# A sixth buffer for split weights, with two weight sums written over loaded weights, in a decoder trunk on one core

## The chip, the cores and the metric

The kernel runs on one core of one Trainium2 chip. The metric is the device time of one execution in microseconds; the kernel before takes 2459.61 us, the median of three runs (2458.16 to 2460.76). One further execution was taken with the profiler on: 2458.1 us, of which the span from the first to the last profiled instruction is 2456.3 us. The rows of the profile are of that execution.

The engines by their names in the profile: PE multiplies matrices (PEld loads its stationary operand), DVE does elementwise work on vectors, ACT copies, casts and evaluates functions, POOL is a slower general engine, and SP issues DMA transfers.

## What is computed

Two layers on 256 tokens of width 2048, all in float32. Layer 0 is RetNet retention (8 heads) and an MLP with squared ReLU; layer 1 is latent attention over a shared key and value (16 heads) and an MLP of the same form.

```python
x = x + retention(rms_norm(x, norm_mix[0]), w_in, w_out, cos, sin)
x = x + square(relu(rms_norm(x, norm_mlp[0]) @ w1)) @ w2
k_nope, k_pe, v = mla_shared_kv(rms_norm(x, kv_norm_in), ...)
x = x + mla_attention(rms_norm(x, norm_mix[1]), ..., k_nope, k_pe, v)
x = x + square(relu(rms_norm(x, norm_mlp[1]) @ w1)) @ w2
```

The weights are some 480 MB and are read once. Nearly all time goes into products of 256 tokens with weight matrices.

## The kernel before

**Split products.** A float32 number is split into a high part (a rounding cast on ACT, line 216) and a low part (number minus high part, a subtraction on DVE, line 217). A product of two split matrices takes three matmuls: high by high, high by low, low by high (lines 409 to 411). Each matmul has 512 columns.

**Quads.** A weight matrix is cut into blocks of 256 by 1024; `quad` (from line 321) handles one. One transfer of 1 MB on SP's queue (line 324) brings it into a tile `raw`, of which there are three. It holds four pieces of 512 columns in the order B11, B22, B12, B21. The tokens stand in two halves and the inner dimension in two, so a quad multiplies two by two pieces by two by two. There are two kinds:

- A plain quad, an *eight*, splits `raw` in two parts of 1024 columns and does eight products (24 matmuls).
- A quad with sums, a *seven*, uses Winograd's form of Strassen's scheme: seven products (21 matmuls) on B11, B22, B21 and four sums of weights, u1 = B11+B12, u3 = B22+B12, u2 = u1+B22 and u4 = u2+B21 (with the signs put into the activations). DVE makes u1 and u3 in one addition (line 363), u2 (line 372) and u4 (line 373), and the four parts are then split in the order (B11, B22), (B21), (u2, u4), (u1, u3). The products follow in that order: p1, c12; c11; c21, p6; p5, p7.

Which quads of a GEMM are sevens is written out by hand (`SEVEN`, `ODD`, `HEAD` and so on): three or four of eight in most GEMMs, two in some.

**Buffers.** Each part has a tile `wh` and a tile `wl` of 1024 columns; there are five of each. The sums of one quad take both places of the tag `us`. A cast into `wh` waits until PE has used the part five places before; a load waits until the last reader of the `raw` three loads before is done; the first sum waits until `us` is free.

**Pairs.** `gemm_pair` runs eight quads into eight PSUM banks (four `acc`, two `tp`, and one double bank for p6 and p7) and then hands them to `pair_out`, where ACT copies c22, c12, c11, c21, p1 and p5 and DVE adds p6 and p7. The next GEMM takes those banks again. There are 16 such pairs for the first MLP matrices (names `u_`) and 16 for the second (`d_`), seven for gates and values of retention (`rp_`), four for its output (`ro_`), and one each in attention's query (`dqp_`) and output (`wop_`). Other GEMMs go through `stream` (line 242), with splits of the same size and without sums.

**Order of the work.** Python code emits everything unrolled; short tasks (evictions, transposes, normalisation, softmax) are put on a list with a due time counted in quads (`later`, `tick`). A scheduler then orders each engine's queue by emission order and readiness and makes the waits. `queued_behind` adds an order between two instructions of one engine: in a seven, the first sum goes behind the first low part of the quad before, and the first low parts go behind the last sum.

**Small things that the change touches.** `gains`, `cst` (inverse frequencies for the rotations, mask of three blocks of 128 columns, identity) and `gpe` are constants loaded at the start, the last two in `start` (lines 684 to 697). `sincos` computes the rotation tables on POOL in a chain of some 25 instructions; `rope_tab` serves the retention heads, `pe_tabs` and the rotated key `kpe_t` serve attention. `small` is a ring of 36 tiles for row statistics, `f2k` a ring of 14 tiles of 2 KB per partition for all else.

Of the kernel before, what the change touches and what calls it, by code (L numbers as in the profile page):

```python
# [35 lines left out]
P = 128  # L36
NT = 2
# [12 lines left out]

G_MIX0, G_MLP0, G_KV, G_MIX1, G_MLP1 = 0, 16, 32, 48, 64
G_CKV, G_CQ, G_KN, G_QN, G_ALL = 80, 84, 96, 97, 98
C_INVR, C_INVM, C_MASK, C_ID, C_ALL = 0, 128, 160, 544, 672

MAGIC = 1.5 * 2.0**23
MAGIC_HI = 1.5 * 2.0**35
# [10 lines left out]
def yoco(ctx: ExitStack, tc: tile.TileContext, a):  # L67
# [5 lines left out]
        return pool.tile([P, *shape], dtype, tag="f2k", bufs=14, name=name)  # L73

    def small(w, name):
        return pool.tile([P, w], F32, tag="small", bufs=36, name=name)

    def shaped(t, shape):
        v = t[:, : math.prod(shape)]
# [33 lines left out]


    gains = pool.tile([P, G_ALL], F32, name="gains")
    cst = pool.tile([P, C_ALL], F32, name="cst")
    pos_i = pool.tile([P, NT], I32, name="pos_i")
    gpe = pool.tile([P, 2 * ROPE], F32, name="gpe")
    nc.scalar.dma_start(gains, a["gains"])
    ident = cst[:, C_ID : C_ID + P]  # L120
    mask = cst[:, C_MASK : C_MASK + 3 * P]
    neg_half = pool.tile([P, 16], F32, name="neg_half")
    nc.gpsimd.memset(neg_half, -0.5)
    warm = small(1, "warm")
    nc.scalar.copy(warm, neg_half[:, 0:1])
# [112 lines left out]
    def stream(w, chunk, cols, name, use, done=None, before=None):  # L238

        raw = pool.tile([P, 2048], F32, tag="raw", bufs=3, name=f"{name}_raw")  # L240
        if before is None:
            nc.sync.dma_start(raw[:, :cols], w[chunk])
        n = cols // 2
        for half in range(2):
            wh = pool.tile([P, 1024], F32R, tag="wh", bufs=5, name=f"{name}_wh{half}")
            wl = pool.tile([P, 1024], F32R, tag="wl", bufs=5, name=f"{name}_wl{half}")
# [74 lines left out]
    def quad(w, chunk, x, mm, name, split_ends=False):  # L321

        raw = pool.tile([P, 2048], F32, tag="raw", bufs=3, name=f"{name}_raw")
        nc.sync.dma_start(raw, w[chunk])
        v, more = x

        def a(t, k):
            return [v[:, k, i, t * P : (t + 1) * P] for i in range(2)]

        def s(n):  # L330
            return [more[:, n // 2, i, n % 2 * P : (n % 2 + 1) * P] for i in range(2)]

        def parts(src, n, part, after=None):
            wh = pool.tile([P, 1024], F32R, tag="wh", bufs=5, name=f"{name}_wh{part}")
            wl = pool.tile([P, 1024], F32R, tag="wl", bufs=5, name=f"{name}_wl{part}")
            low = low_part[0] = split(wh[:, : n * 512], wl[:, : n * 512], src)
            if after is not None:
                queued_behind(low, after)
            if part == 0:
                first_low[0] = low  # L340
            return [[i[:, j * 512 : (j + 1) * 512] for i in (wh, wl)] for j in range(n)]

        if more is None:
            b11, b22 = parts(raw[:, 0:1024], 2, 0)
            if not split_ends:
                mm("c11", a(0, 0), b11)
                mm("c21", a(1, 0), b11)
                mm("c12", a(0, 1), b22)
# [12 lines left out]
            return  # L361
        u = [pool.tile([P, 2, 512], F32, tag="us", bufs=2, name=f"{name}_u{i}") for i in range(2)]
        first_sum = nc.vector.tensor_tensor(
            u[0], raw[:, 0:1024].rearrange("p (i n) -> p i n", i=2),
            raw[:, 1024:1536].unsqueeze(1).to_broadcast([P, 2, 512]), op=ALU.add,
        )
        if first_low[0] is not None:
            queued_behind(first_sum, first_low[0])
        if ahead[1] is not None:
            queued_behind(first_sum, ahead[1])  # L370
            ahead[1] = None
        nc.vector.tensor_tensor(u[1][:, 0], u[0][:, 0], raw[:, 512:1024], op=ALU.add)
        summed_up = nc.vector.tensor_tensor(u[1][:, 1], u[1][:, 0], raw[:, 1536:], op=ALU.add)  # L373
        b11, b22 = parts(raw[:, 0:1024], 2, 0, summed_up)
        mm("p1", a(0, 0), b11)
        mm("c12", s(3), b22)
        (b21,) = parts(raw[:, 1536:], 1, 1, summed_up)
        mm("c11", a(0, 1), b21)
        u2, u4 = parts(u[1].rearrange("p i n -> p (i n)"), 2, 2)
        mm("c21", a(1, 1), u4)  # L380
        mm("p6", s(2), u2)
        u1, u3 = parts(u[0].rearrange("p i n -> p (i n)"), 2, 3)
        mm("p5", s(1), u1)
        mm("p7", s(0), u3)

    def gemm_pair(w, chunk0, act, kinds, name, done, order=None, inner=None, ends=False):

# [216 lines left out]
        return finish  # L604

    scale = (NOPE + ROPE) ** -0.5
    rope_tab = pool.tile([P, 2, S], F32, name="rope_tab")
    pe_tabs = [[pool.tile([P, 2, ROPE], F32, name=f"petab{t}{i}") for i in range(2)] for t in range(NT)]
    gqn = pool.tile([P, 1], F32, name="gqn")

    def mla_tables():
        sm = mla_sc[0](no_turn[0])
# [13 lines left out]

    def ret_tables():
        nc.vector.tensor_copy(pos_f, pos_i)
        ret_sc.append(sincos(cst[:, C_INVR : C_INVR + 128], 128, "tr"))

    def scale_tables():
        r0.extend(x_rstd(ss0, "n0"))
# [51 lines left out]
    def start(half):  # L684
        first_inputs(half)
        if half == 4:
            nc.sync.dma_start(pos_i, a["pos"])
            nc.sync.dma_start(cst, a["cst"])
            nc.sync.dma_start(gpe, a["gpe"])
        if half == 5:  # L690
            ret_tables()
        if half == 7:
            for b in range(NB):
                later(2 + b, lambda b=b: load_x(b))
            later(6, scale_tables)
            later(18, lambda: mla_sc.append(sincos(cst[:, C_INVM : C_INVM + 32], 32, "tm")))
            later(26, mla_tables)

    def ret_rope(acc, out, name, wait):
# [240 lines left out]
    sck = square_sums(2, "sck")  # L940
    spe = square_sums(1, "spe")
    rc, ckv = [], []
    kpe_t = pool.tile([P, 2, S], F32R, name="kpe_t")

    def downed(acc, b):
        need(r2, NT)
# [165 lines left out]
    def score(b, qt, qpe):  # L1112
# [15 lines left out]
        p = [f2k([2, (t + 1) * P], f"p{b}{t}") for t in range(NT)]  # L1128
        for t in range(NT):
            cols = slice(t * P, t * P + (t + 1) * P)  # L1130
            cut = mask[:, cols].unsqueeze(1).to_broadcast([P, 2, (t + 1) * P])
# [83 lines left out]
def _constants():  # L1215
# [10 lines left out]
    cst[:, C_MASK : C_MASK + 3 * P] = np.concatenate([causal, np.zeros((P, P)), causal], axis=1)  # L1226
# [66 lines left out]
```

## Time and profile before

| quantity | value |
|---|---|
| median of three runs | 2459.61 us |
| profiled execution | 2458.1 us |
| its span | 2456.3 us |
| instructions | 31721 |
| HBM read, written | 479.14 MB, 39.85 MB |
| mean DMA rate | 212 GB/s |
| granted TensorE clock | 1.00 in all shown stretches |

How to read the rows: a row of groups has line, engine, operation, output and inputs, shape and count, then busy time in us and the mean of one in ns, then the engine's idle time ahead of them and what ended it. A row of the timeline has start and duration in us. A row of waits has the instruction that waited, whom it waited for, total us, times and the longest. A row of stretches has from and to, the length, the busy time of PE, PEld, DVE, ACT and POOL with the number of instructions, the granted clock, the busy share of DMA and GB/s. A matmul's duration overlaps with the next one's, so busy time of PE is the union of overlapping bars.

### The profile page before, as it was taken

The numbers are of one execution on the slowest core, as the hardware profiler recorded it, in microseconds if no ns is written. First come the engines' busy times: TensorE is split into PE (matmuls) and PEld (weight loads), VectorE is DVE, ScalarE is ACT, GpSimd is POOL, SyncE is SP. The second block draws the span as 40 slices with busy tenths as digits, with TensorE's granted clock in tenths as the row PEclk, the third lists the DMA queues.
The fourth block names the chain that finished last, engine by engine and source line by source line (L and its number), as shares of the span: only waits on it lengthen the run. The fifth ranks groups of instructions, "written<-read, shape, count | busy, mean of one in ns | idle before, by whom it ended". The sixth has DMA issues, their size and how long they took to land.

```text
span 2456.3 us, 31721 instructions
## 1 busy us (share of the span) xinstructions
PE 2446.2 (100%) x11614; PEld 2057.6 (84%) x11614; DVE 2212.2 (90%) x2919; ACT 1641.3 (67%) x2307; POOL 238.0 (10%) x287
## 2 busy tenths in 40 slices
PE   9999999999999999999999999999999999999999
PEld 7888888888888888888888888998888888888887
DVE  7899899888899999999999998777899999999998
ACT  6566666556676767667676777577667667676674
POOL 6400001000000010010110001101000100100100
PEclk9999999999999999999999999999999999999999
DMA  8555569556565586695786555444555865957854
GB/s 309 207 201 191 192 202 259 191 183 224 197 218 194 196 254 218 207 272 187 241 253 213 200 202 180 155 162 173 197 199 205 252 228 194 262 198 229 264 209 170
DMA packets 93692, 521.05 MB, mean 212 GB/s; under 512 B 11104, under 2 KB 12512, under 8 KB 40288
## 3 DMA queue, kind: packets, MB, share of 16 engines
q1 hardware_dynamic: 72144, 472.83, 55.2%
q0 software_dynamic: 21248, 46.15, 8.9%
q8 instruction: 91, 1.49, 0.2%
q14 instruction: 65, 0.53, 0.1%
q10 hardware_dynamic: 144, 0.05, 0.0%
HBM read 479.14 MB, written 39.85 MB: 211 GB/s over the span
## 4 chain that ended last, share of the span: by engine, by line
PE 92%; DVE 2%; ACT 1%; issue 0%; DMA 0%; POOL 0%; ACTq 0%; DVEq 0%
PE u_c L411 7%; PE u_c L410 7%; PE u_c L409 7%; PE d_c L411 6%; PE d_c L410 6%; PE d_c L409 6%; PE rp_c L411 3%; PE rp_c L409 3%; PE rp_c L410 3%; PE u_p L411 2%; PE u_p L410 2%; PE u_p L409 2%; PE rq_acc L307 2%; PE rk_acc L307 2%; PE ro_c L411 2%; PE ro_c L409 2%
## 5 line engine op out<-in xcount | busy, mean ns | idle before, releaser
L217 DVE TENSOR_TENSOR d_wl<-d_raw,d_wh 128x1024 fp32r<-128x1024 f32 (+1 forms) x256 | 278.7, 1111 | 31.6 <-ACT d_wh L216 31.6
L217 DVE TENSOR_TENSOR u_wl<-u_raw,u_wh 128x1024 fp32r<-128x1024 f32 (+1 forms) x256 | 279.3, 1113 | 29.8 <-ACT u_wh L216 29.8
L409 PE MATMUL u_c<-u_wh,n 128*128 128x512 f32 x712 | 278.3, 392 | 0.0
L411 PE MATMUL u_c<-u_wh,n 128*128 128x512 f32 x712 | 277.2, 389 | 0.0
L410 PE MATMUL u_c<-u_wl,n 128*128 128x512 f32 x712 | 277.2, 389 | 0.0
L409 PE MATMUL d_c<-d_wh,hid 128*128 128x512 f32 x706 | 275.4, 392 | 0.5 <-ACT d_wh L216 0.5
L411 PE MATMUL d_c<-d_wh,hid 128*128 128x512 f32 x706 | 275.0, 390 | 0.0
L410 PE MATMUL d_c<-d_wl,hid 128*128 128x512 f32 x706 | 274.8, 389 | 0.0
L216 ACT CAST u_wh<-u_raw 128x1024 fp32r<-128x1024 f32 (+1 forms) x256 | 241.3, 973 | 49.6 <-PE u_c L411 24.1
L216 ACT CAST d_wh<-d_raw 128x1024 fp32r<-128x1024 f32 (+1 forms) x256 | 240.3, 971 | 39.9 <-PE d_c L411 16.6
L216 ACT CAST d_wh<-d_u 128x1024 fp32r<-128x1024 f32 x106 | 108.1, 1051 | 119.7 <-DVE d_u L373 82.6
L216 ACT CAST u_wh<-u_u 128x1024 fp32r<-128x1024 f32 x104 | 106.2, 1052 | 116.0 <-DVE u_u L373 77.3
L411 PEld LDWEIGHTS u_c<-u_wh,n 128*128 128x128 f32 x712 | 133.7, 188 | 27.8
L410 PEld LDWEIGHTS u_c<-u_wl,n 128*128 128x128 f32 x712 | 133.8, 188 | 27.4 <-DVE u_wl L217 0.3
L409 PEld LDWEIGHTS u_c<-u_wh,n 128*128 128x128 f32 x712 | 133.7, 188 | 27.0
L409 PEld LDWEIGHTS d_c<-d_wh,hid 128*128 128x128 f32 x706 | 132.6, 188 | 28.2 <-ACT d_wh L216 1.4
L411 PEld LDWEIGHTS d_c<-d_wh,hid 128*128 128x128 f32 x706 | 132.5, 188 | 27.6
L410 PEld LDWEIGHTS d_c<-d_wl,hid 128*128 128x128 f32 x706 | 132.6, 188 | 27.5 <-DVE d_wl L217 0.4
L216 ACT CAST rp_wh<-rp_raw 128x1024 fp32r<-128x1024 f32 x112 | 103.8, 945 | 74.2 <-PE rp_c L411 49.2
L217 DVE TENSOR_TENSOR rp_wl<-rp_raw,rp_wh 128x1024 fp32r<-128x1024 f32 x112 | 119.7, 1090 | 16.4 <-ACT rp_wh L216 16.2
L217 DVE TENSOR_TENSOR u_wl<-u_u,u_wh 128x1024 fp32r<-128x1024 f32 x104 | 123.5, 1222 | 3.1 <-ACT u_wh L216 2.8
L217 DVE TENSOR_TENSOR d_wl<-d_u,d_wh 128x1024 fp32r<-128x1024 f32 x106 | 125.8, 1221 | 0.0
(570 smaller groups left out, 6505.3 us busy)
## 6 DMA issues: line engine op xcount, KB each, us to landing
u_raw<-in_mlp_w SPq DMA_DIRECT2D x128, 1024.0 KB, 5.4
d_raw<-in_mlp_w SPq DMA_DIRECT2D x128, 1024.0 KB, 4.9
rp_raw<-in_ret_w_gv SPq DMA_DIRECT2D x56, 1024.0 KB, 4.8
ro_raw<-in_ret_w_out SPq DMA_DIRECT2D x32, 1024.0 KB, 4.9
uq_raw<-in_mla_w_uq SPq DMA_DIRECT2D x24, 768.0 KB, 4.3
rq_raw<-in_ret_w_qk SPq DMA_DIRECT2D x16, 1024.0 KB, 4.9
rk_raw<-in_ret_w_qk SPq DMA_DIRECT2D x16, 1024.0 KB, 4.8
xh<-d_c POOLq DMA_DIRECT2D x48, 256.0 KB, 6.1
```

What stands on the lines that cost most here:

```text
L216: nc.scalar.copy(h, src)
L217: return nc.vector.tensor_tensor(l, src, h.bitcast(F32), op=ALU.subtract)
L307: nc.tensor.matmul(acc[f], wh[:, cols], a.rearrange("p i s -> p (i s)"), start=k == 0, stop=k == nk - 1)
L409: nc.tensor.matmul(dst, ah, bh, start=n == 0, stop=False)
L410: nc.tensor.matmul(dst, ah, bl, start=False, stop=False)
L411: nc.tensor.matmul(dst, al, bh, start=False, stop=n == total[key] - 1)
```

## The change

- `wh` and `wl` have six buffers each.
- In a seven, u1 and u3 go into one tile (`us` has one place), u2 is written over B12 in `raw` and u4 over B21, after B21 has been split. The last sum and the parts change places: (B11, B22), (B21), then u4's sum, then (u1, u3), then (u2, u4). The products are now p1, c12; c11; p5, p7; c21, p6. `raw` is read until the last part is split.
- The rotation table, the attention tables and the rotated key share two places (tag `tab`).
- `cst` keeps two blocks of mask and the identity; the inverse frequencies and `gpe` are loaded into `f2k` tiles when they are needed. `small` has 26 tiles instead of 36, `neg_half` 8 columns instead of 16.

```diff
-            wh = pool.tile([P, 1024], F32R, tag="wh", bufs=5, name=f"{name}_wh{part}")
-            wl = pool.tile([P, 1024], F32R, tag="wl", bufs=5, name=f"{name}_wl{part}")
+            wh = pool.tile([P, 1024], F32R, tag="wh", bufs=6, name=f"{name}_wh{part}")
+            wl = pool.tile([P, 1024], F32R, tag="wl", bufs=6, name=f"{name}_wl{part}")
...
-        u = [pool.tile([P, 2, 512], F32, tag="us", bufs=2, name=f"{name}_u{i}") for i in range(2)]
+        u = pool.tile([P, 2, 512], F32, tag="us", bufs=1, name=f"{name}_u")
         first_sum = nc.vector.tensor_tensor(
-            u[0], raw[:, 0:1024].rearrange("p (i n) -> p i n", i=2),
+            u, raw[:, 0:1024].rearrange("p (i n) -> p i n", i=2),
             raw[:, 1024:1536].unsqueeze(1).to_broadcast([P, 2, 512]), op=ALU.add,
         )
...
-        nc.vector.tensor_tensor(u[1][:, 0], u[0][:, 0], raw[:, 512:1024], op=ALU.add)
-        summed_up = nc.vector.tensor_tensor(u[1][:, 1], u[1][:, 0], raw[:, 1536:], op=ALU.add)
+        summed_up = nc.vector.tensor_tensor(raw[:, 1024:1536], u[:, 0], raw[:, 512:1024], op=ALU.add)
         b11, b22 = parts(raw[:, 0:1024], 2, 0, summed_up)
         mm("p1", a(0, 0), b11)
         mm("c12", s(3), b22)
         (b21,) = parts(raw[:, 1536:], 1, 1, summed_up)
         mm("c11", a(0, 1), b21)
-        u2, u4 = parts(u[1].rearrange("p i n -> p (i n)"), 2, 2)
+        last_sum = nc.vector.tensor_tensor(raw[:, 1536:], raw[:, 1024:1536], raw[:, 1536:], op=ALU.add)
+        queued_behind(last_sum, low_part[0])
+        u1, u3 = parts(u.rearrange("p i n -> p (i n)"), 2, 3, last_sum)
+        mm("p5", s(1), u1)
+        mm("p7", s(0), u3)
+        u2, u4 = parts(raw[:, 1024:], 2, 2)
         mm("c21", a(1, 1), u4)
         mm("p6", s(2), u2)
-        u1, u3 = parts(u[0].rearrange("p i n -> p (i n)"), 2, 3)
-        mm("p5", s(1), u1)
-        mm("p7", s(0), u3)
...
-    rope_tab = pool.tile([P, 2, S], F32, name="rope_tab")
-    pe_tabs = [[pool.tile([P, 2, ROPE], F32, name=f"petab{t}{i}") for i in range(2)] for t in range(NT)]
+    rope_tab = pool.tile([P, 2, S], F32, tag="tab", bufs=2, name="rope_tab")
+    pe_tab = pool.tile([P, NT, 2, 2, ROPE], F32, tag="tab", bufs=2, name="pe_tab")
+    pe_tabs = [[pe_tab[:, t, i] for i in range(2)] for t in range(NT)]
...
+    def inverse(lo, n, name):
+        inv = f2k([n], name)
+        nc.sync.dma_start(inv, a["cst"][:, lo : lo + n])
+        return inv
...
-        ret_sc.append(sincos(cst[:, C_INVR : C_INVR + 128], 128, "tr"))
+        ret_sc.append(sincos(inverse(C_INVR, 128, "invr"), 128, "tr"))
...
-            nc.sync.dma_start(cst, a["cst"])
-            nc.sync.dma_start(gpe, a["gpe"])
+            nc.sync.dma_start(cst, a["cst"][:, C_MASK:])
...
-    kpe_t = pool.tile([P, 2, S], F32R, name="kpe_t")
+    kpe_t = pool.tile([P, 2, S], F32R, tag="tab", bufs=2, name="kpe_t")
```

More of the change, by code (lines that the diff above doesn't have):

```diff
@@ L52 @@
 G_CKV, G_CQ, G_KN, G_QN, G_ALL = 80, 84, 96, 97, 98
-C_INVR, C_INVM, C_MASK, C_ID, C_ALL = 0, 128, 160, 544, 672
+C_INVR, C_INVM, C_MASK, C_ID, C_ALL = 0, 128, 160, 416, 544
 MAGIC = 1.5 * 2.0**23
@@ L75, in small @@
     def small(w, name):
-        return pool.tile([P, w], F32, tag="small", bufs=36, name=name)
+        return pool.tile([P, w], F32, tag="small", bufs=26, name=name)
     def shaped(t, shape):
@@ L115, in yoco @@
     gains = pool.tile([P, G_ALL], F32, name="gains")
-    cst = pool.tile([P, C_ALL], F32, name="cst")
+    cst = pool.tile([P, C_ALL - C_MASK], F32, name="cst")
     pos_i = pool.tile([P, NT], I32, name="pos_i")
-    gpe = pool.tile([P, 2 * ROPE], F32, name="gpe")
     nc.scalar.dma_start(gains, a["gains"])
-    ident = cst[:, C_ID : C_ID + P]
-    mask = cst[:, C_MASK : C_MASK + 3 * P]
-    neg_half = pool.tile([P, 16], F32, name="neg_half")
+    mask = cst[:, 0 : 2 * P]
+    ident = cst[:, 2 * P : 3 * P]
+    neg_half = pool.tile([P, 8], F32, name="neg_half")
     nc.gpsimd.memset(neg_half, -0.5)
@@ L244, in stream @@
         for half in range(2):
-            wh = pool.tile([P, 1024], F32R, tag="wh", bufs=5, name=f"{name}_wh{half}")
-            wl = pool.tile([P, 1024], F32R, tag="wl", bufs=5, name=f"{name}_wl{half}")
+            wh = pool.tile([P, 1024], F32R, tag="wh", bufs=6, name=f"{name}_wh{half}")
+            wl = pool.tile([P, 1024], F32R, tag="wl", bufs=6, name=f"{name}_wl{half}")
             cuts = 1
@@ L606, in yoco @@
     scale = (NOPE + ROPE) ** -0.5
-    rope_tab = pool.tile([P, 2, S], F32, name="rope_tab")
-    pe_tabs = [[pool.tile([P, 2, ROPE], F32, name=f"petab{t}{i}") for i in range(2)] for t in range(NT)]
+    rope_tab = pool.tile([P, 2, S], F32, tag="tab", bufs=2, name="rope_tab")
+    pe_tab = pool.tile([P, NT, 2, 2, ROPE], F32, tag="tab", bufs=2, name="pe_tab")
+    pe_tabs = [[pe_tab[:, t, i] for i in range(2)] for t in range(NT)]
     gqn = pool.tile([P, 1], F32, name="gqn")
+    def inverse(lo, n, name):
+        inv = f2k([n], name)
+        nc.sync.dma_start(inv, a["cst"][:, lo : lo + n])
+        return inv
     def mla_tables():
+        gpe = f2k([2 * ROPE], "gpe")
+        nc.sync.dma_start(gpe, a["gpe"])
         sm = mla_sc[0](no_turn[0])
@@ L695, in start @@
             later(6, scale_tables)
-            later(18, lambda: mla_sc.append(sincos(cst[:, C_INVM : C_INVM + 32], 32, "tm")))
+            later(18, lambda: mla_sc.append(sincos(inverse(C_INVM, 32, "invm"), 32, "tm")))
             later(26, mla_tables)
@@ L1130, in score @@
             cols = slice(t * P, t * P + (t + 1) * P)
-            cut = mask[:, cols].unsqueeze(1).to_broadcast([P, 2, (t + 1) * P])
+            cut = mask[:, P - t * P : 2 * P].unsqueeze(1).to_broadcast([P, 2, (t + 1) * P])
             nc.vector.tensor_tensor(p[t], sc[:, :, cols], cut, op=ALU.add)
@@ L1225, in _constants @@
     causal = np.where(i[None, :] <= i[:, None], 0.0, -1e30)
-    cst[:, C_MASK : C_MASK + 3 * P] = np.concatenate([causal, np.zeros((P, P)), causal], axis=1)
+    cst[:, C_MASK : C_MASK + 2 * P] = np.concatenate([np.zeros((P, P)), causal], axis=1)
     cst[:, C_ID : C_ID + P] = np.eye(P)
```

## The prediction

> **What bounds the kernel now.** First the page: busy shares, then the chain that ended last.
>
> ```profile
> PE 2446.2 (100%) x11614; PEld 2057.6 (84%) x11614; DVE 2212.2 (90%) x2919; ACT 1641.3 (67%) x2307; POOL 238.0 (10%) x287
> PE 92%; DVE 2%; ACT 1%; issue 0%; DMA 0%; POOL 0%; ACTq 0%; DVEq 0%
> ```
>
> PE has 10.1 us without work in a span of 2456.3, and 92% of the chain is PE. But matmul durations overlap, so a busy PE may still run late. The timeline of PE shows the real pace, and the table of stretches whether the two MLP stages keep it:
>
> ```profile
> 793.44 0.39 PE L411 MATMUL u_c<-u_wh,n 128*128 128x512 f32 x1
> 793.67 0.39 PE L409 MATMUL u_p<-u_wh,n 128*128 128x512 f32 x1
> 793.89 0.39 PE L410 MATMUL u_p<-u_wl,n 128*128 128x512 f32 x1
> 700.00:1365.00 665.00, 665.00 (x3011) 552.31 (x3010) 619.01 (x737) 459.02 (x596) 50.48 (x65) 1.00 0.69 221
> 1800.00:2370.00 570.00, 570.00 (x2573) 473.31 (x2572) 530.63 (x621) 391.25 (x496) 45.80 (x56) 1.00 0.70 224
> 1370.00:1440.00 70.00, 68.66 (x389) 59.22 (x388) 62.16 (x115) 52.39 (x105) 4.07 (x6) 1.00 0.56 200
> 2415.00:2440.00 25.00, 24.45 (x107) 19.62 (x106) 24.79 (x27) 13.61 (x16) 0.00 (x0) 1.00 0.59 191
> 0.00:35.00 35.00, 32.77 (x137) 23.78 (x138) 24.92 (x36) 24.47 (x42) 16.34 (x17) 1.00 0.88 313
> 95.00:120.00 25.00, 23.89 (x117) 19.56 (x116) 22.35 (x33) 14.64 (x26) 19.30 (x28) 1.00 0.41 147
> ```
>
> A 512-column matmul lasts 0.39 us but the next starts after 0.227 us: that is PE's pace. In 1235 us of MLP it is never idle (665.00 of 665.00, 570.00 of 570.00). Of the idle time 2.2 us lie in the first 35, 1.1 at 95 to 120, 1.3 between the layers and 0.55 at 2415 to 2440; the other 4.9 lie in the attention stages and after the last matmul. A stall shorter than the overlap (0.39 - 0.227 = 0.16 us) stays hidden in "busy", so each real stall is that much longer than its idle:
>
> ```profile
> 2420.36 0.39 PE L409 MATMUL d_c<-d_wh,hid 128*128 128x512 f32 x1
> 2421.08 0.50 PE L409 MATMUL d_c<-d_wh,hid 128*128 128x512 f32 x1 [0.33 <-ACT d_wh L216]
> PE d_c L409 <- ACT d_wh L216: 0.5, 2, 0.3
> PE d_p L409 <- ACT d_wh L216: 0.2, 1, 0.2
> ```
>
> Idle 0.33, late by 0.72 - 0.227 = 0.49 us. Waits of PE for a split weight are these three in all the quads: 0.7 us idle, about 1.2 us late with 0.16 each. That is all that a sixth buffer can buy directly. Even every idle microsecond, 10.1 us, is only 0.4%.
>
> **The change part by part.** The first fence is the view of line 363, whose six groups (the first and the last are shown) count the quads with sums: 53 + 52 + 28 + 12 + 4 + 4 = 153. The second has the work of one, from the groups by shape; the last numbers are idle time and its releaser.
>
> ```profile
> L363 DVE TENSOR_TENSOR d_u<-d_raw x53: 1218/1222/1235, 820.0 to 2432.7; 128x1024 f32<-128x1024 f32 x53
> ...
> L363 DVE TENSOR_TENSOR wop_u<-wop_raw x4: 1218/1220/1220, 1734.1 to 1764.2; 128x1024 f32<-128x1024 f32 x4
> ```
>
> ```profile
> L363 DVE TENSOR_TENSOR u_u<-u_raw 128x1024 f32<-128x1024 f32 x52 | 63.6, 1223 | 6.1 <-DMA u_raw<-in_mlp_w 6.1
> L373 DVE TENSOR_TENSOR u_u<-u_u,u_raw 128x512 f32<-128x512 f32 x52 | 35.9, 691 | 1.3
> L217 DVE TENSOR_TENSOR u_wl<-u_raw,u_wh 128x1024 fp32r<-128x1024 f32 x204 | 246.8, 1222 | 29.8 <-ACT u_wh L216 29.8
> L217 DVE TENSOR_TENSOR u_wl<-u_u,u_wh 128x1024 fp32r<-128x1024 f32 x104 | 123.5, 1222 | 3.1 <-ACT u_wh L216 2.8
> L216 ACT CAST u_wh<-u_raw 128x1024 fp32r<-128x1024 f32 x204 | 210.8, 1062 | 45.7 <-PE u_c L411 21.3 <-ACT u_wh L216 14.8 <-DMA u_raw<-in_mlp_w 5.9
> L216 ACT CAST u_wh<-u_u 128x1024 fp32r<-128x1024 f32 x104 | 106.2, 1052 | 116.0 <-DVE u_u L373 77.3 <-PE u_c L411 38.6
> ```
>
> *Sums in place.* The same three additions remain, and a subtraction costs 1222 ns from either tile, so DVE's work stays: 0 us. The order changes: the last sum (0.69) goes behind the second low part. The first two low parts come 0.69 us earlier, the last two when they did. But the cast of the two late sums (1.05) now waits for that sum, while DVE has one 1.22 us subtraction left to do: the cast ends about when DVE wants it. Behind it on ACT stand the next quad's casts and any evictions, and DVE's subtractions wait for those. I bound this by 0 and 0.1 us per quad, 15 us over 153, against DVE's 244 us idle (2456.3 - 2212.2). PE hides it as long as its lead lasts; 0 taken.
>
> *A sixth buffer.* It lets ACT and DVE run one part further ahead: six matmuls, 1.36 us of PE, in a quad with sums and twelve, 2.72 us, in one without. ACT does wait for PE to free a buffer (21.3 and 38.6 us above); PE feels it only at the three waits. I take 1.2 us gained; bounds 0 and 3.0, the idle of the three places after the start. The Trainium skill (Perfetto Trace Analysis, Optimization Strategy) says that the same gap repeating on the engine that should be saturated can mean too few buffers. PE shows no repeating gap in these rows, so by that rule this term would be 0 and the time 1.2 us more; I keep the three waits, whose releaser is the cast itself.
>
> *Raw weights kept longer.* This is the price. A raw buffer was free after the second low part; now it is free after the fourth. Nearly every load waits for such a release (127 of 128 in the first row, SP's waits; then timelines, and the one load of that window):
>
> ```profile
> SPq L324 <- DVE u_wl L217: 620.7, 127, 11.0
> 782.69 0.69 DVE L217 TENSOR_TENSOR u_wl<-u_raw,u_wh 128x512 fp32r<-128x512 f32 x1
> 783.46 0.33 SPq L324 DMA_DIRECT2D u_raw<-in_mlp_w  x1
> 785.03 1.23 DVE L217 TENSOR_TENSOR u_wl<-u_u,u_wh 128x1024 fp32r<-128x1024 f32 x1
> 788.44 1.23 DVE L363 TENSOR_TENSOR u_u<-u_raw 128x1024 f32<-128x1024 f32 x1
> 791.03 1.82 DVE L217 TENSOR_TENSOR u_wl<-u_raw,u_wh 128x1024 fp32r<-128x1024 f32 x2
> u_raw<-in_mlp_w SPq DMA_DIRECT2D x1, 1024.0 KB, 4.9
> ```
>
> Here the load starts at 783.46, right behind the 512-wide subtraction, takes 4.9 us, and its first sum starts at 788.44, just after landing at 788.35. With the release at the end of the row of 785.03, 786.26, the load lands near 791.2: the first sum is 2.8 us late, and the first low part (791.03 + 1.22 = 792.25 before) 2.8 - 0.69 = 2.1 us, at 794.4, where PE's matmul of 793.89 wants it. That is 0.5 us of stall if nothing else moves; with DVE 1.36 us ahead thanks to the sixth buffer it is none. Behind the waiting load on SP stands only the next load, whose buffer comes free later still; behind the waiting first sum on DVE stand the quad's other sums and low parts. Bounds per such place 0 and 0.5 us; I take 0 in the MLPs. Between the layers there is no such reserve, since the chain there already runs through loads:
>
> ```profile
> 1376.55 0.33 SPq L324 DMA_DIRECT2D d_raw<-in_mlp_w  x1
> 1377.69 1.05 ACT d_wh L216
> 1379.55 1.22 DVE L217 TENSOR_TENSOR d_wl<-d_u,d_wh 128x1024 fp32r<-128x1024 f32 x1
> 1381.55 1.13 DVE d_u L363
> ```
>
> That load would start when the row of 1379.55 ends, at 1380.77 instead of 1376.55, 4.2 us later; but the cast at 1377.69 waited for a buffer, which the sixth one frees up to 2.72 us sooner. Net 1.5 us at most, a gain of as much if the earlier cast wins; I take +0.6.
>
> *Order of products.* c21 and p6 are now last, p5 and p7 before. In the case below (end of a pair) the second of the two copies, at 891.48, is c21's. Its last product would now start 0.9 us before the next pair's 892.71 and end at 892.2, so this copy and the two behind it move by 0.7 us and it ends at 892.8. The next pair's fourth product needs that bank at 894.75: cover 1.9 us, cost 0, and the whole 0.7 per pair if the cover were gone.
>
> ```profile
> 891.00 1.09 ACT L432 COPY d_c<-d_c 128x512 f32<-128x512 f32 x2
> 892.71 0.39 PE L409 MATMUL u_c<-u_wh,n 128*128 128x512 f32 x1
> 894.75 0.39 PE L409 MATMUL u_c<-u_wh,n 128*128 128x512 f32 x1
> ```
>
> *Constants.* The block of 336 KB loses 144; three small loads (64, 16 and 64 KB) come instead of one of 64. SP issues them between weight loads, 0.33 us each, in place of the one issue removed. The frequencies now land behind the block:
>
> ```profile
> 18.15 1.55 POOL L570 TENSOR_SCALAR tr_ang<-cst,pos_f 128x128 f32<-128x128 f32 x2 [17.31 <-DVE pos_f L628]
> 59.55 0.73 POOL L206 TENSOR_TENSOR n_r<-n_m,neg_half 128x2 f32<-128x2 f32 x1 [1.89 <-DVE n_m L205]
> gains<-in_gains ACTq DMA_DIRECT2D x1, 49.0 KB, 2.5
> ```
>
> POOL's angle chain has 1.89 us of reserve before the row that ends it. A load like the gains takes 2.5 us, so the chain slips 0 to 0.6 us beyond it; 144 KB less in a start that moves 313 GB/s (the row 0 to 35) give up to -0.5. I take 0. Fewer small tiles, the shared table places (the rotated key comes after the last use of the rotation table) and the shorter mask can add only single waits on engines beside PE: 0, bounds 0 and 1.
>
> Sum against the profiled execution's own 2458.1 us: -1.2 + 0.6 = -0.6, or 2457.5. The median of the runs shown is 1.5 us above that execution: **2459.0**.
>
> **The rivals.**
>
> A, slower: late loads starve PE. The release moves by 2.9 us in the case shown, and DMA is 0.70 busy in these stretches, so delayed loads also share it. It decides where the delay passes the lead that the sixth buffer gives; against it speaks that lead. Price: 0.5 us at one place in each of the 16 up pairs, and 1.5 at the layers' border: 2459.6 + 9.5, or 2469. With loads that share, 1 us each: 2477.
>
> B, slower by DVE: the 0.1 us per quad grows to 0.3 through evictions. Only stretches where DVE has nothing left, like 2415 to 2440 (24.79 of 25), pass it on; with 20 of the 153 quads in such, 6 us: 2465.6.
>
> C, faster: the lead removes the idle of the three places after the start (3.0 us), with their hidden parts (twelve stalls of 0.16, an estimate: 2), and the fewer bytes of the start 0.5: 2459.6 - 5.5 = 2454.1. Against it: the three waits are the only ones there that end with a weight cast.
>
> D: nothing changes, since three raw buffers and not five split ones limit the lead: 2459.6, inside the forecast.
>
> E: PE's pace itself has slack. Weight loads fill 84% of the span; were the other 16% waits for parts, 393 us could go, to 2067. Against it: the stretch of 665 us has 552.31, or 83%, with PE never idle. The Trainium skill (Perfetto Trace Analysis, Identifying the Most-Contended Engine) judges PE's headroom by this share and not by matmul time; the trace's even pace of 0.227 us disagrees.
>
> **How the numbers follow.** Forecast with D 0.58 (own range 2455 to 2464.5), A 0.22, B 0.05, C 0.14, E 0.01. The bound of 0.2% (about what a measurement of this kernel can tell from no change) is 4.9 us. Faster 0.15, same 0.58, slower 0.27. The range 2453 to 2470 takes in C, B and the middle of A.
>
> **What would show it.** Right: both MLP stretches with PE at their full length, PE's waits for d_wh gone or shorter, ACT's waits for L373 replaced by waits for the last sum. A is shown by idle of PE behind casts or low parts in the MLPs, and by longer waits of L363 for raw; B by DVE waiting for casts of the late sums. A time under 2452 would mean that PE's pace itself had slack.

## The result, and the profile after

The kernel after takes 2475.57 us, the median of six runs (2471.56 to 2483.45), against 2459.91 for the kernel before in as many (2458.16 to 2460.76). The ratio is 1.0069 with a 95% interval of 1.0053 to 1.0085: slower by 0.7%, by more than 0.2%, and above the range of the prediction. The runs of the kernel after also scatter over 12 us, those of before over 2.6. The profiled execution took 2479.43 us, its span is 2477.7. In the kernel after, lines of the helpers stand one lower (the cast is line 215, the low part 216, the load 323, the first sum 362); the last sum, line 373 before, is line 377, the Relu of the hidden blocks line 884, their transposes on PE line 234.

First the busy shares of the page, then the table of stretches for the two MLPs, both of the kernel after:

```profile
PE 2453.5 (99%) x11614; PEld 2058.1 (83%) x11614; DVE 2227.8 (90%) x2919; ACT 1633.4 (66%) x2307; POOL 249.8 (10%) x287
```

```profile
700.00:1365.00 665.00, 657.77 (x2961) 544.06 (x2960) 613.71 (x723) 443.58 (x577) 49.05 (x61) 0.99 0.69 218
1800.00:2370.00 570.00, 565.19 (x2549) 467.65 (x2547) 529.88 (x621) 382.34 (x494) 47.00 (x58) 1.00 0.71 223
```

The MLPs, where PE was never idle, now have 7.2 and 4.8 us without PE. The count says more than the busy time: 2961 + 2549 matmuls where before had 3011 + 2573, so 74 fewer at 0.227 us, or 16.8 us of delay inside the same stretches. That is most of the 21.4 us by which this execution's span is longer. The waits of PE in the kernel after name it (waiting instruction, whom it waited for, total us, times, longest); no such row exists in the kernel before:

```profile
PE hid_tp L234 <- ACT u_c L884: 12.0, 9, 2.5
```

In the MLPs PE does not wait for weights. It waits for the *hidden blocks*: the transposes that follow each pair of the first MLP matrix need the Relus on ACT, and these are late. The nine waits lie at six places (945, 1114, 1287, 2008, 2178 and 2347 us), always behind the first pair of a group (two GEMMs with the first MLP matrix, two with the second), and in six of the eight groups. The chain of the kernel after at the last of these places, in order of time, shows what makes the Relu late:

```profile
2337.10 1.24 DVE u_wl L216
...
2338.35 9.17 DMA u_raw<-in_mlp_w
...
2347.90 0.07 ACT u_wh L215
...
2348.85 0.73 ACT u_c L884
...
2349.63 1.54 PE hid_tp L234 x6
2351.17 0.43 PE u_c L411
```

Read it from the top: the last low part of a quad frees its raw buffer; only then does a load start, and it takes 9.17 us; a cast on ACT stands waiting for it; the Relu stands behind that cast in ACT's queue, though its own inputs are ready; PE stands waiting for the Relu. A prefetch holds up an eviction. DVE's queue has the same kind of hold-up. Two rows of its timeline at this place are a low part that waited for a cast of the load before, ahead of the block sums, and the block sum that the Relu reads, ready at 2347.45:

```profile
2345.03 1.23 DVE L216 TENSOR_TENSOR u_wl<-u_raw,u_wh 128x1024 fp32r<-128x1024 f32 x1 [0.77 <-ACT u_wh L215]
2346.77 0.68 DVE L448 TENSOR_TENSOR u_c<-u_c,u_u 128x512 f32<-128x512 f32 x1
```

The timeline of ACT in the kernel after at another of the places (start, duration, then in brackets idle before and releaser):

```profile
1281.02 1.10 ACT L432 COPY u_p<-u_p 128x512 f32<-128x512 f32 x2
1283.96 2.00 ACT L215 CAST u_wh<-u_raw 128x1024 fp32r<-128x1024 f32 x2 [1.84 <-DMA u_raw<-in_mlp_w]
1285.87 0.72 ACT L884 ACTIVATE u_c<-u_c,n_r 128x512 f32<-128x512 f32 x1
1288.34 1.04 ACT L215 CAST u_wh<-u_raw 128x1024 fp32r<-128x1024 f32 x1 [1.76 <-DMA u_raw<-in_mlp_w]
1289.29 0.72 ACT L884 ACTIVATE u_c<-u_c,n_r 128x512 f32<-128x512 f32 x1
1289.91 0.60 ACT L215 CAST u_wh<-u_raw 128x512 fp32r<-128x512 f32 x1
1290.42 1.33 ACT L884 ACTIVATE u_c<-u_c,n_r 128x512 f32<-128x512 f32 x2
```

Between the last copy and the last Relu ACT is idle for 1.84 + 1.76 = 3.6 us, all of it ahead of casts that wait for loads. (The profile's chain at this place runs through a transfer of `x_mlp` to the DVE sum of 1287.39 instead; DVE has no idle time ahead of that sum, so that transfer did not hold it up.) The same stretch of work in the kernel before, one pair's end, has casts among the Relus too, and no bracket:

```profile
1270.03 1.10 ACT L216 CAST u_wh<-u_raw 128x1024 fp32r<-128x1024 f32 x1
1270.98 0.77 ACT L877 ACTIVATE u_c<-u_c,n_r 128x512 f32<-128x512 f32 x1
1271.60 2.99 ACT L216 CAST u_wh<-u_raw 128x1024 fp32r<-128x1024 f32 x3
1274.44 2.22 ACT L877 ACTIVATE u_c<-u_c,n_r 128x512 f32<-128x512 f32 x3
```

There is a second cost behind each long stall. The table of stretches of the kernel after around 1290 us (from and to, length, busy PE, PEld, DVE, ACT, POOL, then the granted clock, DMA's share and GB/s):

```profile
1286.00:1290.00 4.00, 1.33 (x6) 0.47 (x4) 4.00 (x7) 2.24 (x4) 0.00 (x0) 1.00 1.00 411
1290.00:1292.00 2.00, 1.94 (x10) 1.65 (x11) 1.55 (x2) 2.00 (x5) 0.00 (x0) 0.73 0.65 180
1292.00:1294.00 2.00, 2.00 (x6) 1.60 (x5) 1.17 (x3) 1.75 (x4) 0.00 (x0) 0.50 0.88 356
1294.00:1296.00 2.00, 2.00 (x9) 1.64 (x8) 2.00 (x5) 1.15 (x2) 0.00 (x0) 0.92 0.30 119
```

After 2.5 us without work the granted clock is 0.73, then 0.50, and is back by 1296; PE is busy all the while and starts a matmul every 0.43 us instead of 0.227.

Worked out from the starts of successive matmuls in both kernels (each interval less 0.227 us), the spans' difference of 21.4 us splits so: 13.7 us ahead of hidden transposes, 2.4 at half clock, 1.0 elsewhere between the first and the last matmul of the two MLPs, and 4.3 outside them, nearly all of it ahead of the first MLP.

### The profile page after: what moved, and what is told of

It is laid out like the page before. It is cut to its first block, busy times and chain, and to the rows that moved or that the text cites. A ratio compares the mean times of both kernels' runs of the same rounds, so it can differ in the third digit from the quotient of the medians.

```text
span 2477.7 us, 31766 instructions
## 1 busy us (share of the span) xinstructions
PE 2453.5 (99%) x11614; PEld 2058.1 (83%) x11614; DVE 2227.8 (90%) x2919; ACT 1633.4 (66%) x2307; POOL 249.8 (10%) x287
## 4 chain that ended last, share of the span: by engine, by line
PE 83%; DVE 8%; DMA 5%; ACT 2%; issue 2%; POOL 0%; SPq 0%; ACTq 0%; DVEq 0%
PE d_c L411 6%; PE d_c L410 6%; PE d_c L409 6%; PE u_c L411 6%; PE u_c L409 6%; PE u_c L410 6%; DMA u_raw<-in_mlp_w 3%; PE rp_c L409 2%; PE rp_c L411 2%; PE rp_c L410 2%; PE rq_acc L306 2%; PE d_p L410 2%; PE d_p L411 2%; PE d_p L409 2%; PE u_p L410 1%
## 5 line engine op out<-in xcount | busy, mean ns | idle before, releaser
L215 ACT CAST u_wh<-u_raw 128x1024 fp32r<-128x1024 f32 (+1 forms) x308 | 293.1, 980 | 170.1 <-DVE u_raw L377 91.2
L215 ACT CAST d_wh<-d_raw 128x1024 fp32r<-128x1024 f32 (+1 forms) x309 | 293.8, 982 | 125.1 <-DVE d_raw L377 77.2
L216 DVE TENSOR_TENSOR u_wl<-u_raw,u_wh 128x1024 fp32r<-128x1024 f32 (+1 forms) x308 | 340.2, 1129 | 33.7 <-ACT u_wh L215 21.6
L216 DVE TENSOR_TENSOR d_wl<-d_raw,d_wh 128x1024 fp32r<-128x1024 f32 (+1 forms) x309 | 341.1, 1127 | 24.9 <-PE u_c L409 13.5
L215 ACT CAST rp_wh<-rp_raw 128x1024 fp32r<-128x1024 f32 (+1 forms) x140 | 133.1, 965 | 115.3 <-PE rp_c L411 56.7
L216 DVE TENSOR_TENSOR rp_wl<-rp_raw,rp_wh 128x1024 fp32r<-128x1024 f32 (+1 forms) x140 | 153.8, 1118 | 14.8 <-ACT rp_wh L215 13.6
L151 POOL DMA_DIRECT2D xh<-d_c x48 | 41.7, 868 | 795.5 <-ACT d_c L432 611.1
L409 PE MATMUL rp_c<-rp_wh,a 128*128 128x512 f32 x280 | 109.7, 392 | 1.7 <-DVE rk_u L711 1.7
L411 PE MATMUL rp_c<-rp_wh,a 128*128 128x512 f32 x280 | 109.2, 390 | 0.0
L410 PE MATMUL rp_c<-rp_wl,a 128*128 128x512 f32 x280 | 109.0, 389 | 0.0
```

What stands on the lines that cost most here:

```text
L151: ins = nc.gpsimd.dma_start(x_home[t][2 * p + j], c[t][j][i], accum_op=ALU.add)
L215: nc.scalar.copy(h, src)
L216: return nc.vector.tensor_tensor(l, src, h.bitcast(F32), op=ALU.subtract)
L409: nc.tensor.matmul(dst, ah, bh, start=n == 0, stop=False)
L410: nc.tensor.matmul(dst, ah, bl, start=False, stop=False)
L411: nc.tensor.matmul(dst, al, bh, start=False, stop=n == total[key] - 1)
```

## Experiments

Three theories went into the runs. **L**: the raw buffer is kept to the last part, so loads start and land late. **Q**: the sixth buffer lets ACT and DVE take up casts of a later load ahead of the Relus, and these wait for the load; the order in the queue is the cause. **O**: c21 and p6 now end a quad, so the pair's last evictions are late by themselves. The comparisons are with the kernel before on the same chip (2459.6 to 2459.9 us).

**b5: the kernel after with five buffers** (the same edit also in `stream`, which serves the other GEMMs).

```diff
-            wh = pool.tile([P, 1024], F32R, tag="wh", bufs=6, name=f"{name}_wh{part}")
-            wl = pool.tile([P, 1024], F32R, tag="wl", bufs=6, name=f"{name}_wl{part}")
+            wh = pool.tile([P, 1024], F32R, tag="wh", bufs=5, name=f"{name}_wh{part}")
+            wl = pool.tile([P, 1024], F32R, tag="wl", bufs=5, name=f"{name}_wl{part}")
```

> The changed kernel with five buffers for the split parts again; sums over loaded weights, the new order of products and the small constants stay. Theory Q (the sixth buffer lets the casts of a later load go ahead of the evictions in ACT's queue, and they wait there for the load): back to 2460 to 2464 us, and PE's waits for the hidden transposes under 2 us. Theory L (a raw buffer kept until the fourth part makes loads late, whatever the number of buffers): 2470 to 2480 us. Theory O (c21 and p6 last make the evictions late): 2468 to 2475 us.

Measured: 2468.71 us (2466.95 to 2472.62), ratio 1.0039 [1.0024, 1.0054]. About half of the loss stays without the sixth buffer. PE's waits in this kernel:

```profile
PE hid_tp L234 <- ACT u_c L884: 5.3, 6, 1.9
PE u_c L409 <- ACT u_c L432: 2.1, 2, 1.7
```

It is the same wait, smaller, and once PE waits for a copy of the pair itself. Q alone cannot be it; L and O remain for this half, though the time lies 1.3 us below the range given for L.

**order_old: the kernel after with the old order of parts and products.** The sums stay in place, but (u2, u4) are split and multiplied before (u1, u3).

```diff
-        u1, u3 = parts(u.rearrange("p i n -> p (i n)"), 2, 3, last_sum)
-        mm("p5", s(1), u1)
-        mm("p7", s(0), u3)
-        u2, u4 = parts(raw[:, 1024:], 2, 2)
+        u2, u4 = parts(raw[:, 1024:], 2, 2, last_sum)
         mm("c21", a(1, 1), u4)
         mm("p6", s(2), u2)
+        u1, u3 = parts(u.rearrange("p i n -> p (i n)"), 2, 3)
+        mm("p5", s(1), u1)
+        mm("p7", s(0), u3)
```

> The changed kernel with the old order of parts and products (u2 and u4 before u1 and u3; c21 and p6 before p5 and p7); six buffers and the sums over loaded weights stay, the raw buffer is free one subtraction earlier. Theory O: 2458 to 2463 us. Theory Q: no better than 2468 us. Theory L: between, 2464 to 2472 us, since the release moves by 1.1 of its 2.9 us.

Measured: 2572.54 us (2570.55 to 2573.61), ratio 1.0458 [1.0442, 1.0473]; L and O missed it by 100 us, and Q had only a lower bound. The edit brings in a wait of its own. The waits of this kernel:

```profile
PE d_c L409 <- ACT d_wh L215: 18.3, 20, 1.1
PE u_c L409 <- ACT u_wh L215: 7.7, 19, 0.8
ACT d_wh L215 <- DVE d_raw L377: 205.9, 45, 9.3
```

With u4 written over B21 its sum must wait until B21 is split; if the next part to be split is the one with u4, then low part, sum, cast and low part of one quad run one after the other. ACT waits 205.9 us for those sums in the second MLP matrices alone (77.2 in the kernel after), and PE waits for weights in both. So here the new order is what lets the sums be made in place. The run says nothing on O.

**small_only: only the small things** (tables that share places, constants in pieces, 26 small buffers), with five buffers and the quads of before.

> Only the small parts of the change (constants, shared tables, fewer small tiles); five buffers and sums in tiles of their own as before. All three theories: 2459 to 2461 us, no difference. If it is over 2463 us, the late constants cost something at the start.

Measured: 2462.91 us (2461.91 to 2464.49), ratio 1.0014 [1.0004, 1.0023]: 3.3 us slower, not the nothing that was expected. The stalls are single ones in other stages, such as these of PE:

```profile
PE rq_acc L302 <- DVE rq_wl L216: 2.0, 2, 1.1
PE n_tp L234 <- DVE n L218: 1.2, 1, 1.2
```

**wh6_own: small_only with a sixth high buffer alone** (five low ones, sums in their own tiles, loads released as before).

```diff
-            wh = pool.tile([P, 1024], F32R, tag="wh", bufs=5, name=f"{name}_wh{part}")
+            wh = pool.tile([P, 1024], F32R, tag="wh", bufs=6, name=f"{name}_wh{part}")
```

> Sums in tiles of their own and the old order, as before; six buffers for the high parts and five for the low parts, with the small parts of the change. The raw buffer is free after the second low part again. Theory Q: slower than before, 2464 to 2472 us, since the casts go ahead of the evictions as in the changed kernel. Theories L and O: 2457 to 2461 us.

Measured: 2469.55 us (2466.07 to 2470.59), ratio 1.0037 [1.0022, 1.0052], 6.6 us above small_only. A further buffer for cast weights by itself costs time and brings back the wait ahead of the hidden transposes. That is in Q's range; L and O, with no load kept longer and the old order of products, did not expect it. Its waits:

```profile
PE hid_tp L234 <- ACT u_c L883: 4.0, 2, 2.0
ACT u_wh L215 <- DMA u_raw<-in_mlp_w: 7.7, 6, 2.2
```

**hold_casts: the kernel after with the casts held back.** The casts of the two quads after the next, their first sum and low parts are put behind the last Relu (ACT) and the last sum of the blocks (DVE).

```diff
+            if hold is not None:
+                queued_behind(cast[0], hold[0])
+                queued_behind(low, hold[1])
...
+                turn_first[:] = [[last_relu, last_added[0], 3]]
```

> The kernel after (six buffers, sums in place, small parts as after) with one thing more: in the queues of ACT and DVE the casts, the first sum and the low parts of the two quads whose turn comes after the next one stand behind the last Relu and the last sum of the hidden blocks, as five buffers had kept them. Theory Q (the sixth buffer lets casts that still wait for their load go ahead of the Relus): the waits of PE's hidden transposes for ACT's Relu (12.0 us in 9) and the slow matmuls behind them go, 2461 to 2466, near the 2462.9 of the small parts alone. Theory L (raw buffers kept longer, loads late): loads stay as late, the waits move to the weight parts, 2469 to 2477. Theory O (products c21 and p6 last): Relus still late by their own evictions, waits of 1 to 1.5 us at each of the eight places stay, 2468 to 2474.

Measured: 2475.34 us (2473.78 to 2477.55), ratio 1.0064 [1.0051, 1.0076]. The wait ahead of the transposes is gone (0.8 us in two), and the time is the same. That is the figure of L, but the run cannot be read so, because of its sister below. Nor does it restore the order of five buffers: in all 16 pairs the four Relus have one, two, three and three casts fewer ahead of them than in b5.

**b5_raw4: five buffers and a fourth raw buffer.** The 8 KB of the sixth pair go to a load that may run ahead; order, sums in place and small things are those of the kernel after.

```diff
-        raw = pool.tile([P, 2048], F32, tag="raw", bufs=3, name=f"{name}_raw")
+        raw = pool.tile([P, 2048], F32, tag="raw", bufs=4, name=f"{name}_raw")
...
-            wh = pool.tile([P, 1024], F32R, tag="wh", bufs=6, name=f"{name}_wh{part}")
+            wh = pool.tile([P, 1024], F32R, tag="wh", bufs=5, name=f"{name}_wh{part}")
```

> The kernel after with five high and five low buffers, as before, and a fourth raw buffer in the place of the sixth (same memory): loads have one buffer more to run ahead, though each is still kept to the last part. Theory L (the raw buffer kept longer is what remains of the loss with five buffers, 2468.7): waits of ACT and DVE for raw loads fall to some 10 us or less, 2460 to 2464. Theory O: nothing of the evictions changes, 2466 to 2470. Theory Q says of it only what the order in the queues is: that of five buffers, so waits as with five, 2466 to 2470.

Measured: 2459.00 us (2458.51 to 2459.53), ratio 0.9996 [0.9987, 1.0005]. The whole loss is gone, that of the small things too. That is L's direction, 1 us below its range. The MLP stretches:

```profile
700.00:1365.00 665.00, 665.00 (x3011) 551.30 (x3011) 620.40 (x736) 454.12 (x593) 50.72 (x63) 1.00 0.70 221
1800.00:2370.00 570.00, 570.00 (x2572) 472.35 (x2571) 532.27 (x621) 387.34 (x496) 45.83 (x56) 1.00 0.72 225
```

PE is never idle, with 3011 and 2572 matmuls as before. ACT and DVE have no wait for a raw MLP load at all. O is refuted: c21 and p6 are last here as well.

**b5_raw4_hold: both remedies at once.**

> Five high and low buffers, four raw buffers, and the casts and low parts held behind the Relus as in hold_casts: both suspected causes are taken away at once. If Q and L are all there is beside the small parts: 2460 to 2464. If O has a part of its own (c21 and p6 last make the evictions late whatever stands between): 2466 to 2470.

Measured: 2475.73 us (2474.86 to 2476.11), ratio 1.0064 [1.0051, 1.0076]; 16.7 us above b5_raw4, with loads in time, and outside both ranges. So holding the casts back costs as much as it was to save. The stretches of this kernel, then PE at one place:

```profile
700.00:1365.00 665.00, 663.42 (x2974) 543.09 (x2973) 614.17 (x725) 444.47 (x581) 49.64 (x61) 1.00 0.68 218
1800.00:2370.00 570.00, 568.58 (x2544) 465.31 (x2543) 527.08 (x616) 378.26 (x487) 45.82 (x56) 1.00 0.70 222
```

```profile
957.77 0.39 PE L425 MATMUL u_c<-u_wh,n 128*128 128x512 f32 x1
958.00 0.63 PE L423 MATMUL u_p<-u_wh,n_more 128*128 128x512 f32 x2
958.71 0.49 PE L423 MATMUL u_c<-u_wh,n 128*128 128x512 f32 x1
959.32 0.50 PE L424 MATMUL u_p<-u_wl,n_more 128*128 128x512 f32 x1
```

65 matmuls fewer than b5_raw4 in the same stretches, 14.8 us, and only 3.0 of it as idle time. With casts and low parts held back, PE's own queue changed as well, in 16 places: three products with high parts first (958.00 to 958.71), then the low parts. In this kernel each of the 16 comes out some 0.77 us late. hold_casts therefore changed two things, and its wait for Q's order cannot be told from the price of the hold.

**halves: each raw buffer cut in two.** Six half buffers of 4 KB and two loads of 512 KB per quad; six cast buffers stay. The first half is free after the quad's first part. ACT's queue at the ends of the pairs is the one of the kernel after, cast by cast.

```diff
-        raw = pool.tile([P, 2048], F32, tag="raw", bufs=3, name=f"{name}_raw")
-        nc.sync.dma_start(raw, w[chunk])
+        raw, raw2 = [pool.tile([P, 1024], F32, tag="raw", bufs=6, name=f"{name}_raw{i}") for i in range(2)]
+        nc.sync.dma_start(raw, w[chunk][:, 0:1024])
+        nc.sync.dma_start(raw2, w[chunk][:, 1024:2048])
```

> The kernel after with each load's 8 KB buffer cut in two of 4 KB, each with a load of its own (six halves in the place of three wholes, same memory): the first half comes free after the first part of the quad, only the second is kept to the last one. Six high and low buffers stay, and the casts stand ahead of the Relus in ACT's queue exactly as in the kernel after (two casts of u_12 ahead of the first Relu). Theory L (loads that land late are what is needed for the loss; the order in the queue only hands the wait on): waits of ACT and DVE for raw loads fall well below the 65 us of after, hidden transposes wait under 3 us, 2459 to 2464. Theory Q (the order in the queue by itself makes the Relus late): waits of the hidden transposes stay near 12 us, 2470 to 2477.

Measured: 2461.02 us (2460.33 to 2462.66), ratio 1.0004 [0.9995, 1.0013]. ACT in this kernel, at the place shown above for the kernel after:

```profile
1275.65 1.11 ACT L434 COPY u_p<-u_p 128x512 f32<-128x512 f32 x2
1276.60 2.05 ACT L215 CAST u_wh<-u_raw 128x1024 fp32r<-128x1024 f32 x2
1278.50 0.77 ACT L886 ACTIVATE u_c<-u_c,n_r 128x512 f32<-128x512 f32 x1
1279.13 1.08 ACT L215 CAST u_wh<-u_raw 128x1024 fp32r<-128x1024 f32 x1
1280.73 0.73 ACT L886 ACTIVATE u_c<-u_c,n_r 128x512 f32<-128x512 f32 x1 [0.52 <-DVE u_c L450]
1281.36 0.61 ACT L215 CAST u_wh<-u_raw 128x512 fp32r<-128x512 f32 x1
1281.93 1.34 ACT L886 ACTIVATE u_c<-u_c,n_r 128x512 f32<-128x512 f32 x2
```

The same two casts ahead of the first Relu, the same one ahead of the second, and no wait for a load: from the start of the last two copies to the end of the last Relu 7.6 us (1275.65 to 1283.27) instead of 10.7 (1281.02 to 1291.75). With loads in time the order is harmless. What six buffers then gain is nothing that can be measured.

**small26, tabs_only, consts_only: the small things apart**, each on the kernel before: 26 small buffers alone; those and the shared places; the constants in pieces alone.

> The kernel before with one number changed: 26 small buffers in the place of 36. It asks which of the small parts costs the 3.3 us of small_only. If the small buffers do (norms and sums of squares wait for a free one): 2461.5 to 2464. If the constants and tables loaded in pieces do: 2459 to 2460.5, no difference.

> The kernel before with the shared table places and 26 small buffers, constants loaded whole as before. If the sharing of tables is what costs 3 us in small_only: 2461.5 to 2464. If the constants loaded in pieces are: 2459 to 2460.5.

> The kernel before with the constants loaded in pieces as in the kernel after (inverse frequencies and the rotary table fetched when they are used, a narrower mask), tables and small buffers as before. If the later loads of constants cost the 3 us of small_only: 2461.5 to 2464. If the sharing of tables does: 2459 to 2460.5. If both this and tabs_only come out at 2459 to 2460.5, the 3 us are no property of a part.

Measured: 2459.46 us, 0.9998 [0.9989, 1.0007]; 2460.54 us, 1.0002 [0.9993, 1.0011]; 2461.36 us, 1.0006 [0.9998, 1.0015]. None differs from before beyond its interval, and consts_only lies between the two ranges given for it; together they fall short of the 3.3 us of small_only by about 1 us. Which part costs them stays open. They are no fixed price, since b5_raw4 has all of these parts and loses nothing.

**All of it in one measure.** For each of the 256 MLP loads I took from the trace the time from its landing to the start of the first cast of it on ACT (the first half, for halves), and set beside it PE's wait ahead of the hidden transposes. These come from the one profiled execution of each kernel (2479.4 us for after, 2472.6 for b5, 2466.1 for wh6_own); the time is the median of all runs.

| kernel | raw, cast buffers | median slack, us | loads with under 0.5 us | PE waits for Relus, us | time, us |
|---|---|---|---|---|---|
| before | 3, five | 4.8 | 18 | 0 | 2459.9 |
| small_only | 3, five | 4.6 | 21 | 0 | 2462.9 |
| wh6_own | 3, six high | 3.9 | 17 | 4.0 | 2469.6 |
| b5 | 3, five | 2.9 | 42 | 5.3 | 2468.7 |
| after | 3, six | 2.9 | 40 | 12.0 | 2475.6 |
| halves | six halves, six | 6.6 | 1 | 0 | 2461.0 |
| b5_raw4 | 4, five | 7.5 | 0 | 0 | 2459.0 |

The loss needs two things at one place: a load that has not landed, and a cast of it ahead of evictions in ACT's queue. A raw buffer kept longer makes the first (small_only to b5, slack 4.6 to 2.9 us). A further cast buffer makes the second: in wh6_own no more loads are late than in small_only, but in ACT's queue casts stand one place earlier among the Relus, in all 16 pairs; b5 and after have the same slack, and with the casts one place earlier, again in all 16, the loss nearly doubles. The step from small_only to b5 is not clean: with the new order of parts the four Relus also have two, no, one and one casts more ahead of them. So neither L nor Q alone accounts for all rows. That late loads are needed is shown twice: halves keeps the six buffers and the order of after, b5_raw4 the five and the order of b5; both land their loads in time, and the loss is gone. That the order is needed as well is not shown in the same way, since the kernels with the casts held back changed PE's order too.

## Why the prediction was wrong

*What bounds the kernel.* Right: PE's pace in the MLPs is the bound, and the versions with loads in time come back to it (2459.0, 2461.0).

*Sums in place,* 0 us taken. Right: b5_raw4 has them and 0.9996. That ACT's casts would wait for the last sum came true (77.2 us in the second MLP matrices) and is hidden. It is the new order of parts that hides it: with the old one the kernel after is 97 us slower still (order_old).

*A sixth buffer,* 1.2 us gained, bounds 0 and 3.0. Wrong in sign. The three waits that it was to remove are gone (no such row in after, wh6_own or halves, 0.9 us in b5 and b5_raw4), but I treated lead as free; wh6_own makes it 6.6 us worse, since a cast that may be taken up earlier stands in the queue earlier, whether its load is there or not. The lower bound of 0 had no reason behind it.

*Raw weights kept longer,* "I take 0 in the MLPs", 0 to 0.5 us per place. **This is the step that failed.** The working was right up to the late landing, 2.8 us in its example; the median slack fell by 1.9. It then asked only whether PE would get its weights in time, and for what stood behind the waiting first sum on DVE. It never listed what stands behind the waiting *cast* on ACT. Behind it stand the Relus, and behind those PE. (The term on the sums names evictions behind a cast, but prices them at 0.1 us per quad without a row of a pair's end.) In place of 0 the kernel after has 12.0 us of PE's waits for Relus and 2.4 us at half clock; b5, which has this term without the sixth buffer, is 9.1 us slower than before, the small things included. The 0.6 us taken between the layers does not show: from 1385 to 1455, about the same work as 1370 to 1440 before, PE has 1.2 us without work against 1.3. These are the rows that the step should have been checked against, of the kernel before and then of the kernel after:

```profile
ACT u_wh L216 <- DMA u_raw<-in_mlp_w: 5.9, 5, 2.0
```

```profile
ACT u_wh L215 <- DMA u_raw<-in_mlp_w: 29.3, 26, 2.4
DVE u_u L362 <- DMA u_raw<-in_mlp_w: 17.7, 16, 3.0
```

The lead that the sixth buffer was to give as cover did the opposite.

*Order of products,* 0 with a cover of 1.9 us. The number is right (b5_raw4), but the cover was that of the next pair's bank only. The chain from the copies to the Relus and the transposes was not looked at; in the kernel before it had no reserve to speak of at the place shown: the second Relu (the first of the three in the row of 1274.44) ends at 1275.21 and PE starts the first transpose at 1275.27.

*Constants,* 0 with bounds -0.5 and 0.6, small tiles 0 to 1. small_only measured 3.3 us with a lower end of 1.0; the cause stays open, as above.

*The rivals.* A had the right start, late loads, and the wrong end: it let them starve PE of weights, at 2469, or 2477 with loads that share. They starved it of activations, with stalls of up to 2.5 us and a slower clock behind them; that 2477 lies near the measured time is luck. D said that three raw buffers set the lead, not five split ones: that is what b5_raw4 and halves show, yet D put it at no change. B: DVE's waits for casts of the late sums cost nothing, since b5_raw4 has them too. C: no kernel shows its time. E got no support: no version went below PE's pace.

## What to carry to other kernels

A further buffer between two stages helps only if the stage before it has slack; here it pulled prefetches forward to where they waited. For each prefetch that may come late, list what stands behind it in its engine's queue, evictions above all, and follow that to the bound engine. When memory allows one more buffer, ask which hand-over has the least slack (landing to first use, release to load): here the same 8 KB per partition, added to b5, cost 7 us as a sixth pair of split buffers and won 10 us as a fourth load buffer.

## What the runs showed of the hardware

*The clock after a stall.* At three idle times of 2.1 to 2.5 us the granted clock fell to half and came back within 6 us; at idle times of 1.2 and 1.5 us (945 and 2178) it stayed at 1.00. PE in the kernel after, at the place of the chain:

```profile
2349.63 1.54 PE L234 MATMUL hid_tp<-cst,u_c 128*128 128x128 f32 x6 [2.10 <-ACT u_c L884]
...
2351.39 0.63 PE L409 MATMUL u_c<-u_wh,n 128*128 128x512 f32 x1
2351.82 0.63 PE L410 MATMUL u_c<-u_wl,n 128*128 128x512 f32 x1
2352.24 0.50 PE L411 MATMUL u_c<-u_wh,n 128*128 128x512 f32 x1
2352.58 0.40 PE L409 MATMUL u_c<-u_wh,n 128*128 128x512 f32 x1
```

The slow matmuls last 0.63 us and start 0.43 apart. Three places have such intervals, twelve in all, 2.4 us; the kernel before has them only in its first microseconds. The Trainium skill (TensorE: Matmul & The Clock Gate, Part 1: The HAM clock gate) says that the array's clock is halved after an idle window of about 3.4 us and gives 426.7 ns from start to start for 512 columns then. The trace agrees on the 0.43 us; its idle times of 2.1 to 2.5 us, each a few us behind a shorter one, were enough.

*Loads that overlap.* A load of 1 MB took 4.9 us in the prediction's example and 9.17 us in the chain above. Around 1280 us the kernel after issues loads at 1275.95 and 1279.08, which land at 1283.88 and 1288.24, beside POOL's transfers of `x_mlp`; from 1286 to 1290 DMA is busy throughout. Late loads that overlap are each slower still, which the working with one load of 4.9 us left out. In the first pair of the six groups with stalls a load of the kernel after took 5.99 to 8.75 us (medians by group), against 5.32 and 5.90 in the two groups without; beside those six POOL sends the sums of the group before (`xh`, nine transfers against four). That these transfers make the loads long was not tested by itself. b5_raw4 has loads of 6.6 to 8.5 us at the same six places and no loss, so a long load costs nothing there when it may start early enough.
